# Low parts of the MLP's down weights formed by an adding DMA instead of a VectorE subtraction

## The chip, the cores and the metric

The kernel runs on one core of a Trainium2 chip, in one launch. The metric is device time in microseconds of that core: the median of repeated runs. A profile of one execution gives the order and the durations of the instructions. In the views, PE is TensorE, PEld its weight loads, DVE VectorE, ACT ScalarE, POOL GpSimd and SP SyncE, which here only issues DMAs.

## What is computed

A decoder trunk of two layers over 512 tokens of 1024 channels. Each layer has a token mixer (a linear recurrence with pooling in the first, a convolution module in the second), a cross-attention into 256 memory tokens, and a gated MLP with a short causal convolution. The part that the change touches is the MLP:

```python
def conv_ffn(x, norm, w_up, dw_w, dw_b, w_down):
    h = rms_norm(x, norm) @ w_up
    g = causal_dwconv(h[..., :D_FF], dw_w, dw_b)   # width 3, D_FF = 3072
    u = h[..., D_FF:]
    return (jax.nn.gelu(g) * u) @ w_down
```

It is called once in each layer, and its result is added to the residual stream.

## The kernel before

Activations lie with channels on the 128 partitions and the 512 tokens along the free dimension; `X[c]` is chunk c of 8. All large products keep float32 accuracy by splitting each operand into a high part, rounded to the matmul's fp32r format, and a low part, the remainder. `mm3` then issues three matmuls for each pair of 128x128 weights and 128x512 activations: high by high (L165), high by low (L166), low by high (L167).

Weights come as tiles of 128x1024 float32 (512 KB). `load_w` takes a tile through four steps: SP loads it into one of 3 `raw` buffers; ACT copies it, rounding, into one of 4 `whi` buffers (L159); DVE, or POOL where the caller says so, forms `wlo = raw - whi` in one of 4 `wlo` buffers (L160); PE uses both. A `raw` buffer comes free when the subtraction has read it, a `whi` and a `wlo` buffer when the last matmul of their tile is done. One weight tile is worth 24 matmuls of width 512 in the MLP.

The order on each engine is set at build time by a scheduler that takes the instructions by priority; weight loads carry a priority `AHEAD = 100` in front of their place in the code, so that a tile's load, copy and subtraction stand on their queues ahead of the work of earlier tiles. Every queue is then run in that order, and an instruction that waits holds up all that stands behind it on its engine.

`ffn` runs the MLP in `NG = 6` groups of `GC = 4` channel chunks. `up(c)` makes chunk c: one tile of gate weights, then DVE scales the result (L472), ACT and DVE do the convolution and the GELU (L475, L477, L478), POOL multiplies by the norm's scale (L479); one tile of the other half's weights, whose result DVE multiplies in (L481), and a split of the product. `down(g)` multiplies group g by its down weights: 4 tiles, each for two chunks of `X`, added by DVE (L492). The program's order is four `up`, then `down` of the group before: 8 up tiles, then 4 down tiles, and so on. The first layer ends with a further `down` for the last group, after four tiles for the second layer's attention are loaded; the second layer ends instead with `finish`, which has its own loop and its own `load_w` calls for the last group's 4 down tiles.

Of the kernel before, what the change touches and what calls it, by code (L numbers as in the profile page):

```python
# [10 lines left out]
F32 = mybir.dt.float32  # L11
F32R = mybir.dt.float32r
AF = mybir.ActivationFunctionType
ALU = mybir.AluOpType

P = 128
T = 512
D = 1024
C = D // P
# [4 lines left out]
NG = 6  # L24
GC = CF // NG
EPS = 1e-6
AHEAD = 100
# [28 lines left out]
def trunk(ctx: ExitStack, tc: tile.TileContext, I: dict, out: bass.AP):  # L56
    nc = tc.nc
    V, A, G, PE = nc.vector, nc.scalar, nc.gpsimd, nc.tensor
# [5 lines left out]
    wp = ctx.enter_context(tc.tile_pool(name="w", bufs=4))  # L64
# [8 lines left out]
    def nm(s):  # L73
        uid[0] += 1
        return f"{s}_{uid[0]}"
# [13 lines left out]
    def tmp_f(n=T):  # L89
        return tmp.tile([P, n], F32, tag="tmp", name=nm("tmp"))  # L90
# [9 lines left out]
    def mm_ps():  # L100

        wide[1] += 1
        return aux_ps() if wide[0] and wide[1] % 7 in (2, 5) else main_ps()
# [13 lines left out]
    def col(name, i=0):  # L117
        j = _COL[name] + i
        return par[:, j : j + 1]
# [16 lines left out]
    for t in range(16):  # L136
        G.memset(invt[:, t : t + 1], 1.0 / (t + 1))


    def load_w(src=None, eng=None, raw=None, parts=1, ahead=AHEAD, park=False):  # L140

        with tc.high_priority(0 if raw is not None else ahead):
            if raw is None:
                raw = wp.tile([P, D], F32, tag="raw", name=nm("raw"), bufs=3)
                nc.sync.dma_start(raw, src)
            if park:
                both = [split(raw[:, i : i + T], None, None, eng) for i in (0, T)]
                return [b[0] for b in both], [b[1] for b in both]
            hi = wp.tile([P, D], F32R, tag="whi", name=nm("whi"))
            lo = wp.tile([P, D], F32R, tag="wlo", name=nm("wlo"))  # L150
            n = D // parts
            for i in range(0, D, n):
                split(raw[:, i : i + n], hi[:, i : i + n], lo[:, i : i + n], eng)
        return hi, lo

    def split(src, hi=None, lo=None, eng=None):
        hi = act_r() if hi is None else hi
        lo = act_r() if lo is None else lo
        A.activation(hi, src, AF.Copy)  # L159
        (eng or V).tensor_tensor(lo, src, hi.bitcast(F32), op=ALU.subtract)  # L160
        return hi, lo

    def mm3(ps, w, x, first, last):
        (wh, wl), (xh, xl) = w, x
        PE.matmul(ps, wh, xh, start=first, stop=False)  # L165
        PE.matmul(ps, wh, xl, start=False, stop=False)  # L166
        PE.matmul(ps, wl, xh, start=False, stop=last)  # L167

    def blk(w, i, n=P):
        hi, lo = w  # L170
        if isinstance(hi, list):
            hi, lo, i = hi[i // T], lo[i // T], i % T
        return hi[:, i : i + n], lo[:, i : i + n]
# [100 lines left out]
    def project(w, i, xs):  # L274
        ps = mm_ps()
        for k in range(C):
            mm3(ps, blk(w, k * P), xs[k], k == 0, k == C - 1)
        if Norm.due:
            Norm.due.r = rstd(Norm.due.ss)
            Norm.due = None  # L280
        return ps
# [183 lines left out]
    def ffn(layer, norm, nxt, mem=None):  # L465
        ys = {}

        def up(c):
            ps = project(load_w(I["wup"][(layer * 2) * CF + c]), c, norm.x)
            g = tmp_f(T + 2)  # L470
            G.memset(g[:, :2], 0.0)  # L471
            V.tensor_tensor(g[:, 2:], ps, norm.r, op=ALU.mult)  # L472
            y = tmp_f()
            dw = lambda j: col("f_dw_w", (layer * 3 + j) * CF + c)
            A.activation(y, g[:, 2:], AF.Identity, scale=dw(2), bias=col("f_dw_b", layer * CF + c))  # L475
            for j in (1, 0):
                V.scalar_tensor_tensor(y, g[:, j : j + T], dw(j), y, op0=ALU.mult, op1=ALU.add)  # L477
            A.activation(y, y, AF.Gelu_apprx_tanh)  # L478
            G.tensor_tensor(y, y, norm.r, op=ALU.mult)  # L479
            ps = project(load_w(I["wup"][(layer * 2 + 1) * CF + c]), c, norm.x)  # L480
            V.tensor_tensor(y, ps, y, op=ALU.mult)  # L481
            ys[c] = split(y)

        def down(g):
            for j in range(C // 2):
                w = load_w(I["wdown"][(layer * NG + g) * (C // 2) + j])
                for i in range(2):
                    n = 2 * j + i
                    ps = mm_ps()
                    for k in range(GC):  # L490
                        mm3(ps, blk(w, k * 2 * P + i * P), ys[g * GC + k], k == 0, k == GC - 1)
                    V.tensor_tensor(X[n], X[n], ps, op=ALU.add)  # L492
                    if g == NG - 1:
                        nxt.feed(n)

        for g in range(NG):
            for c in range(g * GC, (g + 1) * GC):
                up(c)
            if g:
                down(g - 1)  # L500
                if mem and g == 1:
                    mem.operand(0)
                    mem.operand(1)
                    mem.outputs()
        if nxt:
            parked = [mem.key_piece(n, park=True) for n in range(KE)]
            down(NG - 1)
            return parked
        else:
            finish([ys[(NG - 1) * GC + k] for k in range(GC)])  # L510

    def finish(y):

        w = [load_w(I["wdown"][(2 * NG - 1) * (C // 2) + j]) for j in range(C // 2)]
        H = T // 2
        for t in (0, H):
            xs, ss, st = [x[:, t : t + H] for x in X], None, stat_ps()[:, :H]
            for n in range(C):
                ps = mm_ps()[:, :H]
                for k in range(GC):  # L520
                    mm3(ps, blk(w[n // 2], (k * 2 + n % 2) * P), blk(y[k], t, H), k == 0, k == GC - 1)
                V.tensor_tensor(xs[n], xs[n], ps, op=ALU.add)
                sq = tmp_f(H)
                A.activation(sq, xs[n], AF.Square)
                if ss is not None and n < C - 1:
                    V.tensor_tensor(sq, sq, ss, op=ALU.add)
                if n >= C - 2:
                    PE.matmul(st, onesf, sq, start=n == C - 2, stop=n == C - 1)
                ss = sq
            r = scale_of(st, H)  # L530
            for n in range(C):
                g = col("final_norm", n)
                if n in (1, 4):
                    A.activation(xs[n], xs[n], AF.Copy, scale=g)
                    G.tensor_tensor(xs[n], xs[n], r, op=ALU.mult)
                else:
                    V.scalar_tensor_tensor(xs[n], xs[n], g, r, op0=ALU.mult, op1=ALU.mult)
                if n % 2:
                    o = out[n - 1 : n + 1, :, t : t + H].rearrange("c p t -> p c t")
                    (nc.sync, A)[n // 2 % 2].dma_start(o, xall[:, n - 1 : n + 1, t : t + H])  # L540
# [340 lines left out]
    raw = [wp.tile([P, D], F32, tag="raw", name=nm("raw"), bufs=3) for _ in range(2)]  # L881
# [97 lines left out]
```

## Time and profile before

| | |
|---|---|
| median of 3 runs | 1494.37 us (1493.18 to 1495.32) |
| the profiled execution's own time | 1493.2 us |
| its span in the profile | 1491.4 us |
| granted TensorE clock, mean over the span | 0.998 |
| PE busy | 1471.6 us (99%), 6982 matmuls |
| DVE busy | 919.2 us (62%) |
| ACT busy | 637.7 us (43%) |
| POOL busy | 201.1 us (13%) |
| DMA | 156.25 MB, mean 105 GB/s |
| weight-tile loads of `wdown` | 48 of 512 KB |

A group row of the profile has the line, the engine, the operation, output and inputs, shapes and count, then busy time and mean duration, then how long the engine stood idle just before such instructions and what ended the wait. A timeline row has the start, the duration, the engine, the line and the operation, with the idle time before it in brackets.

### The profile page before, as it was taken

To read this page: it belongs to the slowest core of one execution; us is meant where nothing else is said; L and a number is where in the kernel's file an instruction comes from. 1 tells how busy PE (TensorE), PEld (TensorE's weight loads), DVE (VectorE), ACT (ScalarE), POOL (GpSimd) and SP (SyncE) were. 2 spreads that over 40 slices of the span, in tenths; PEclk is the share of its full clock that TensorE was granted. 3 is DMA by queue.
4 is the path that set the end of the run, shared out by engine and by line. 5 is a ranking of instruction groups with operands and counts; after the bars stand their busy time and mean duration, and the time that the engine had idled before them with its cause. 6 is when DMAs were issued, how large, how long until landed. Compare 5 with 4: busy or idle time off the path is not lost.

```text
span 1491.4 us, 17877 instructions
## 1 busy us (share of the span) xinstructions
PE 1471.6 (99%) x6982; PEld 1211.2 (81%) x6982; DVE 919.2 (62%) x1230; ACT 637.7 (43%) x891; POOL 201.1 (13%) x227
## 2 busy tenths in 40 slices
PE   8999999999999999999999999999999999999997
PEld 7988788888888888888887666888888888888886
DVE  7877774647655545455666996666565554545556
ACT  7568753435432323323435347444443332323333
POOL 0002300000110101001006862200001010101000
PEclk9999999999999999999999999999999999999999
DMA  7523343213333223333416553321232233333221
GB/s 275 159 87 99 113 127 91 72 37 114 99 99 97 92 95 99 100 99 99 153 46 180 161 150 118 99 86 56 85 99 92 94 97 100 99 99 99 91 79 57
DMA packets 47478, 156.25 MB, mean 105 GB/s; under 512 B 5281, under 2 KB 7329, under 8 KB 47393
## 3 DMA queue, kind: packets, MB, share of 16 engines
q1 hardware_dynamic: 46160, 154.05, 33.4%
q8 instruction: 55, 0.90, 0.2%
q10 hardware_dynamic: 1232, 1.06, 0.2%
q14 instruction: 31, 0.25, 0.1%
HBM read 144.60 MB, written 2.10 MB: 98 GB/s over the span
## 4 chain that ended last, share of the span: by engine, by line
PE 88%; issue 4%; DVE 3%; ACT 2%; POOL 2%; DMA 1%; SPq 0%; DVEq 0%; POOLq 0%; ACTq 0%
PE mm L165 27%; PE mm L166 27%; PE mm L167 27%; PE aux L166 1%; PE aux L165 1%; PE aux L167 1%; PE aux L756 1%; DVE wlo L160 1%; POOL tmp L611 1%; ACT whi L159 1%; DMA raw<-in_wv 1%; PE aux L415 0%; DVE big L587 0%; POOL act L160 0%; DMA big<-in_mem 0%
## 5 line engine op out<-in xcount | busy, mean ns | idle before, releaser
L167 PE MATMUL mm<-act,wlo 128*128 128x512 f32 (+1 forms) x1829 | 705.4, 386 | 2.5 <-DVE wlo L160 2.5
L165 PE MATMUL mm<-act,whi 128*128 128x512 f32 (+1 forms) x1829 | 706.2, 387 | 0.0
L166 PE MATMUL mm<-act,whi 128*128 128x512 f32 (+1 forms) x1829 | 705.4, 386 | 0.4 <-DVE act L160 0.4
L159 ACT ACTIVATE whi<-raw 128x1024 fp32r<-128x1024 f32 x259 | 274.0, 1060 | 575.2 <-PE mm L166 475.7
L165 PEld LDWEIGHTS mm<-act,whi 128*128 128x128 f32 x1829 | 343.7, 188 | 73.9 <-issue 3.3
L167 PEld LDWEIGHTS mm<-act,wlo 128*128 128x128 f32 x1829 | 343.7, 188 | 72.0 <-DVE wlo L160 3.3
L166 PEld LDWEIGHTS mm<-act,whi 128*128 128x128 f32 x1829 | 343.8, 188 | 69.5 <-DVE act L160 1.3
L160 DVE TENSOR_TENSOR wlo<-raw,whi 128x1024 fp32r<-128x1024 f32 x239 | 296.6, 1243 | 65.5 <-ACT whi L159 62.7
L479 POOL TENSOR_TENSOR tmp<-tmp,r 128x512 f32<-128x512 f32 x48 | 62.0, 1292 | 637.5 <-ACT tmp L478 632.6
L492 DVE TENSOR_TENSOR x<-x,mm 128x512 f32<-128x512 f32 x88 | 60.5, 687 | 96.8 <-PE mm L167 96.8
L472 DVE TENSOR_TENSOR tmp<-mm,r 128x512 f32<-128x512 f32 x48 | 33.2, 692 | 125.3 <-PE mm L167 125.2
L481 DVE TENSOR_TENSOR tmp<-mm,tmp 128x512 f32<-128x512 f32 x48 | 33.2, 691 | 95.5 <-POOL tmp L471 87.2
L781 DVE SCALAR_TENSOR_TENSOR aux<-h,par,aux 128x491 f32<-128x491 f32 (+16 forms) x106 | 71.9, 727 | 2.1 <-PE aux L756 1.1
L477 DVE SCALAR_TENSOR_TENSOR tmp<-tmp,par,tmp 128x512 f32<-128x512 f32 x96 | 71.9, 749 | 1.9 <-issue 0.2
L478 ACT ACTIVATE tmp<-tmp 128x512 f32<-128x512 f32 x48 | 30.3, 632 | 95.5 <-DVE tmp L477 95.5
L160 POOL TENSOR_TENSOR wlo<-raw,whi 128x1024 fp32r<-128x1024 f32 x20 | 49.2, 2467 | 123.2 <-ACT whi L159 123.0
L159 ACT ACTIVATE act<-tmp 128x512 fp32r<-128x512 f32 x84 | 52.6, 630 | 23.4 <-DVE tmp L623 7.1
L160 DVE TENSOR_TENSOR act<-tmp,act 128x512 fp32r<-128x512 f32 x84 | 59.9, 716 | 4.1 <-ACT act L159 4.0
L471 POOL MEMSET tmp<- 128x2 f32 x48 | 4.8, 100 | 298.3 <-DVE tmp L195 298.3
L475 ACT ACTIVATE tmp<-tmp,par 128x512 f32<-128x512 f32 x48 | 38.5, 803 | 0.6 <-DVE tmp L472 0.6
L779 POOL TENSOR_TENSOR actf<-actf,tmp 128x499 f32<-128x499 f32 (+7 forms) x28 | 36.3, 1296 | 11.5 <-ACT actf L775 10.2
L166 PE MATMUL aux<-act,whi 128*128 128x512 f32 x79 | 30.8, 389 | 0.0
(214 smaller groups left out, 1290.8 us busy)
## 6 DMA issues: line engine op xcount, KB each, us to landing
raw<-in_wup SPq DMA_DIRECT2D x96, 512.0 KB, 3.5
raw<-in_wdown SPq DMA_DIRECT2D x48, 512.0 KB, 3.6
raw<-in_pw SPq DMA_DIRECT2D x24, 512.0 KB, 4.1
raw<-in_win SPq DMA_DIRECT2D x20, 512.0 KB, 3.6
raw<-in_wv SPq DMA_DIRECT2D x16, 512.0 KB, 5.0
raw<-in_wk SPq DMA_DIRECT2D x16, 512.0 KB, 3.6
raw<-in_wq SPq DMA_DIRECT2D x16, 512.0 KB, 3.6
raw<-in_wo SPq DMA_DIRECT2D x16, 512.0 KB, 3.6
```

The lines of the kernel that those rows point to most:

```text
L159: A.activation(hi, src, AF.Copy)
L160: (eng or V).tensor_tensor(lo, src, hi.bitcast(F32), op=ALU.subtract)
L165: PE.matmul(ps, wh, xh, start=first, stop=False)
L166: PE.matmul(ps, wh, xl, start=False, stop=False)
L167: PE.matmul(ps, wl, xh, start=False, stop=last)
L472: V.tensor_tensor(g[:, 2:], ps, norm.r, op=ALU.mult)
L475: A.activation(y, g[:, 2:], AF.Identity, scale=dw(2), bias=col("f_dw_b", layer * CF + c))
L477: V.scalar_tensor_tensor(y, g[:, j : j + T], dw(j), y, op0=ALU.mult, op1=ALU.add)
L479: G.tensor_tensor(y, y, norm.r, op=ALU.mult)
L492: V.tensor_tensor(X[n], X[n], ps, op=ALU.add)
L779: G.tensor_tensor(z[:, s:], z[:, s:], f[:, s:], op=ALU.add)
L781: V.scalar_tensor_tensor(ps[:, s:], h[:, : T - s], tap(s, c), ps[:, s:], op0=ALU.mult, op1=ALU.add)
```

## The change

A new helper `load_summed` takes the place of `load_w` for the tiles of `down`. It loads `raw` and forms `whi` as before. For the low part, ACT copies `raw` with a factor of -1 into the `wlo` buffer, rounding, which gives minus the high part; then an adding DMA, issued by POOL, adds the unrounded weights onto it in place. Its source is the `raw` tile in the first layer, and the weights in memory, read a second time, in the second layer. `finish` keeps `load_w`.

```diff
+    def load_summed(src, again):
+
+        with tc.high_priority(AHEAD):
+            raw = wp.tile([P, D], F32, tag="raw", name=nm("raw"), bufs=3)
+            nc.sync.dma_start(raw, src)
+            hi = wp.tile([P, D], F32R, tag="whi", name=nm("whi"))
+            lo = wp.tile([P, D], F32R, tag="wlo", name=nm("wlo"))
+            A.activation(lo, raw, AF.Copy, scale=-1.0)
+            G.dma_start(lo, src if again else raw, accum_op=ALU.add)
+            A.activation(hi, raw, AF.Copy)
+        return hi, lo
...
         def down(g):
             for j in range(C // 2):
-                w = load_w(I["wdown"][(layer * NG + g) * (C // 2) + j])
+                w = load_summed(I["wdown"][(layer * NG + g) * (C // 2) + j], layer)
```

It applies to 24 tiles in the first layer (6 groups of 4) and 20 in the second (5 groups of 4). Lines of `ffn` lie 12 further down in the changed kernel (L471 becomes L483, L479 L491). The orders of PE and SP are the same as before, name for name and step for step. What moves is on ACT, POOL and DVE.

On ACT, at the first group's down tiles of the first layer: `whi_3799` to `whi_3901` are the four high parts before, `tmp_3679` and `tmp_3755` the GELU chains of chunks 6 and 7. Before:

```order
L159 ACTIVATE whi_3799<-raw_3797 128x1024
L475 ACTIVATE tmp_3679<-tmp_3676,par 128x512
L478 ACTIVATE tmp_3679<-tmp_3679 128x512
L159 ACTIVATE whi_3833<-raw_3831 128x1024
L159 ACTIVATE act_3717<-tmp_3679 128x512
L159 ACTIVATE whi_3867<-raw_3865 128x1024
L475 ACTIVATE tmp_3755<-tmp_3752,par 128x512
L478 ACTIVATE tmp_3755<-tmp_3755 128x512
L159 ACTIVATE whi_3901<-raw_3899 128x1024
```

And now, where L149 is the high part and L147 the negated copy:

```order
L149 ACTIVATE whi_3799<-raw_3797 128x1024
L147 ACTIVATE wlo_3800<-raw_3797 128x1024
L487 ACTIVATE tmp_3679<-tmp_3676,par 128x512
L490 ACTIVATE tmp_3679<-tmp_3679 128x512
L149 ACTIVATE whi_3834<-raw_3832 128x1024
L147 ACTIVATE wlo_3835<-raw_3832 128x1024
L171 ACTIVATE act_3717<-tmp_3679 128x512
L149 ACTIVATE whi_3869<-raw_3867 128x1024
L147 ACTIVATE wlo_3870<-raw_3867 128x1024
L487 ACTIVATE tmp_3755<-tmp_3752,par 128x512
L490 ACTIVATE tmp_3755<-tmp_3755 128x512
L149 ACTIVATE whi_3904<-raw_3902 128x1024
```

Each down tile's negated copy stands right behind its high part, so one more copy stands ahead of a chunk's GELU chain.

On POOL, at the same place, before:

```order
L471 MEMSET tmp_3752 128x2
L479 TENSOR_TENSOR tmp_3679<-tmp_3679,r_3218 128x512
L471 MEMSET tmp_3992 128x2
L479 TENSOR_TENSOR tmp_3755<-tmp_3755,r_3218 128x512
L471 MEMSET tmp_4068 128x2
```

And now:

```order
L483 MEMSET tmp_3752 128x2
L148 DMA wlo_3800<-raw_3797 128x1024
L491 TENSOR_TENSOR tmp_3679<-tmp_3679,r_3218 128x512
L148 DMA wlo_3835<-raw_3832 128x1024
L483 MEMSET tmp_3996 128x2
L148 DMA wlo_3870<-raw_3867 128x1024
L491 TENSOR_TENSOR tmp_3755<-tmp_3755,r_3218 128x512
L148 DMA wlo_3905<-raw_3902 128x1024
L483 MEMSET tmp_4072 128x2
```

The four adding DMAs now stand among the multiplications of chunks 6 and 7, each waiting there for its tile's negated copy on ACT. In the second layer the same rows read `in_wdown` in place of `raw`. DVE loses the 44 subtractions of these tiles, which stood between the instructions of `up` and `down`.

## The prediction

> **What bounds the kernel now.** First the page's totals, with PE's row of the 40 slices:
>
> ```profile
> PE 1471.6 (99%) x6982; PEld 1211.2 (81%) x6982; DVE 919.2 (62%) x1230; ACT 637.7 (43%) x891; POOL 201.1 (13%) x227
> ...
> PE   8999999999999999999999999999999999999997
> ```
>
> Then PE's own waits (who waited for whom: total, times, longest, in us), of which these two are for low parts of weights:
>
> ```profile
> PE mm L167 <- DVE wlo L160: 3.1, 3, 1.4
> ...
> PE mm L166 <- DVE wlo L160: 1.4, 3, 0.5
> ```
>
> And a table by stage, to see whether PE ever waits where the change works; after the stretch and its length each row has the busy time of five engines, the granted clock and the DMA engines' share:
>
> ```profile
> core 0: us, PE busy (x) PEld busy (x) DVE busy (x) ACT busy (x) POOL busy (x), PEclk, DMA share, GB/s
> 0.00:340.00 340.00, 333.01 (x1612) 279.37 (x1613) 236.84 (x342) 197.05 (x298) 29.64 (x51) 1.00 0.36 116
> 340.00:740.00 400.00, 400.00 (x1766) 331.35 (x1765) 222.01 (x266) 141.47 (x172) 34.45 (x50) 1.00 0.34 105
> 740.00:1060.00 320.00, 316.99 (x1661) 248.19 (x1660) 222.42 (x325) 151.58 (x237) 101.68 (x74) 1.00 0.37 107
> 1060.00:1440.00 380.00, 380.00 (x1678) 314.73 (x1677) 207.49 (x248) 133.08 (x160) 32.10 (x48) 1.00 0.32 100
> 1440.00:1491.40 51.40, 41.60 (x271) 37.52 (x269) 30.49 (x53) 14.51 (x27) 3.21 (x4) 0.94 0.16 52
> ```
>
> PE is the bound. Rows two and four of the table are the two MLPs without their ends: 400.00 of 400 and 380.00 of 380 us busy, at a clock of 1.00. The modelled ends of matmuls can hide very short gaps, but no wait for a subtraction: those are 3.1 and 1.4 us in all, six times, and PE's missing time lies in the other three stretches. So nothing that makes a low part ready earlier in the MLP can bring the end forward; only something that makes it late can move it.
>
> How early a low part is ready is read from the timeline of one down group of the first layer, here ACT (the high parts and two steps of the GELU chain), DVE, POOL and SP.
>
> ```profile
> 632.15 1.06 ACT L159 ACTIVATE whi<-raw 128x1024 fp32r<-128x1024 f32 x1 [3.68 <-PE mm L166]
> 633.12 0.80 ACT L475 ACTIVATE tmp<-tmp,par 128x512 f32<-128x512 f32 x1
> 635.96 0.63 ACT L478 ACTIVATE tmp<-tmp 128x512 f32<-128x512 f32 x1 [2.04 <-DVE tmp L477]
> 637.59 1.06 ACT L159 ACTIVATE whi<-raw 128x1024 fp32r<-128x1024 f32 x1 [1.00 <-PE mm L166]
> ...
> 643.03 1.06 ACT L159 ACTIVATE whi<-raw 128x1024 fp32r<-128x1024 f32 x1 [3.68 <-PE mm L166]
> ...
> 648.48 1.06 ACT L159 ACTIVATE whi<-raw 128x1024 fp32r<-128x1024 f32 x1 [1.01 <-PE mm L166]
> ...
> 653.91 1.06 ACT L159 ACTIVATE whi<-raw 128x1024 fp32r<-128x1024 f32 x1 [3.46 <-PE mm L166]
> ...
> 633.25 1.23 DVE L160 TENSOR_TENSOR wlo<-raw,whi 128x1024 fp32r<-128x1024 f32 x1 [0.23 <-ACT whi L159]
> ...
> 636.67 1.29 POOL L479 TENSOR_TENSOR tmp<-tmp,r 128x512 f32<-128x512 f32 x1 [9.55 <-ACT tmp L478]
> ...
> 634.50 0.33 SPq L145 DMA_DIRECT2D raw<-in_wdown  x1
> ```
>
> The five high parts are D0 to D3, the group's down tiles, and the next up tile. Each waits for PE to release the buffer of the tile four places earlier, so each start marks the end of a tile on PE: 637.59, 643.03, 648.48, 653.91, one tile every 5.44 us. D0's buffer came free at 632.15; three more tiles run before D0, which therefore starts at 648.48. Its low part enters with the third matmul, two of 24 later: 648.48 + 2 x 5.44/24 = 648.93. It was ready at 633.25 + 1.23 = 634.48. That is a cover of 14.4 us, and the same for every tile of the MLP, since every tile keeps this pace.
>
> **The change part by part.** The prices are from these rows of the page:
>
> ```profile
> L159 ACT ACTIVATE whi<-raw 128x1024 fp32r<-128x1024 f32 x259 | 274.0, 1060 | 575.2 <-PE mm L166 475.7
> L160 DVE TENSOR_TENSOR wlo<-raw,whi 128x1024 fp32r<-128x1024 f32 x239 | 296.6, 1243 | 65.5 <-ACT whi L159 62.7
> q1 hardware_dynamic: 46160, 154.05, 33.4%
> raw<-in_wdown SPq DMA_DIRECT2D x48, 512.0 KB, 3.6
> actf<-h SPq DMA_DIRECT2D x32, 256.0 KB, 4.9
> ```
>
> *Removed.* 44 subtractions on DVE, 44 x 1.243 = 54.7 us. DVE is 222.01 of 400 us busy in the first MLP and PE does not wait for it: worth 0.
>
> *Added on ACT.* 44 copies, 44 x 1.06 = 46.6 us, onto 141.47 of 400 and 133.08 of 380 us. The copy for D0 stands ahead of L475, which began at 633.12 and would begin at about 634.2. The chain L475, L477, L478, L479 and L481 of that chunk moves by 1.1 us with it. Behind L481 waits the release of one PSUM bank of five, and five products of two to a tile take over 10 us: 0. If that cover were gone, it would be 1.1 us for each of 22 chunks.
>
> *Added on POOL.* 44 DMA issues. The trace shows none by POOL; SP's issue row has 0.33 us, POOL's own longest step here 1.29 us. I take 1.3. Behind an issue that waits stand L479 and L471 of later chunks. But what D0's issue waits for, its copy, ends at 634.2, before the 636.67 at which L479 could start, and D1's and D3's copies end near 639.7 and 650.6, between two L479. Nothing that PE needs soon is behind them: 0.
>
> *Moved: when the low part is ready.* Call T the time from the end of the negated copy to the landing of the sum, POOL's issue included. High part and copy run back to back, so D0's copy ends at 632.15 + 2 x 1.03, some 634.2, and the sum must land by 648.93: **T up to 14.7 us costs nothing** in the second layer. In the first the adding DMA also holds `raw`. D3's load is issued when D0's tile is let go: in the SP row at 634.50, right behind the subtraction's end at 634.48. It would be issued at 634.2 + T and land 3.6 later. D3's high part could then start at the later of 648.48 and 637.8 + T, its copy end 2.1 after, its sum land T after that; three tiles after its buffer came free its matmuls begin, and the sum is needed at 648.48 + 16.3 + 0.45 = 665.2. So 637.8 + 2.1 + 2T may reach 665.2: **T up to 12.65 us costs nothing** in the first layer.
>
> *What T is.* No row shows an adding DMA. From below: it moves no less than a load of the same tile, 3.6 us. From above: a copy within the on-chip memory, `actf<-h`, takes 4.9 us for 256 KB; two such for 512 KB are 9.8, and twice that, since two operands are read, is 19.6. Near the lower end I take 2 x 3.6 = 7.2, because size, shape and row length are those of the load and two operands are read where the load reads one; with 1.3 for the issue, T = 8.5 us (an estimate), from 4.9 to 20.9. 8.5 lies below both limits, so the sum is 0. The Trainium skill, "Collectives: The Full Stack", section "Part 3: Why 7× under link rate — side-by-side accounting", says that a reduce in the DMA engines runs at half the copy's rate because two sources are read, not because of the addition; by it only the transfer doubles, T would be 3.6 + 1.7 + 1.3 = 6.6 us, and the sum 0 as well; no adding DMA in this trace can confirm it.
>
> *DMA traffic.* 33.4% of 1491.4 us for 154.05 MB is 1.70 us of all 16 engines for one 512 KB tile (0.524 MB). A group of 12 tiles takes 65.3 us and 12 x 1.70 = 20.4 us of the engines; four adds at twice 1.70 bring it to 34. The second read from memory falls in the same account. Room is left: 0.
>
> Sum: 0 us on the profiled execution's own 1493.2 (span 1491.4 and 1.8 around it), which lies 1.2 below the median shown. So the median stays: **1494.4 us**. Its own band, for repeat scatter (1493.18 to 1495.32) and a stray start-up wait of the first adds, is 1492.5 to 1496.5.
>
> **The rivals.**
>
> *The sum lands late (slower).* The place is PE's third matmul of a down tile; it decides from T = 12.65 us in the first layer and 14.7 in the second. At T = 16, D0 is late by 1.3 and D3 of the first layer lands at 637.8 + 2.1 + 32 = 671.9, late by 6.7 against 665.2. That is 6.7 x 6 groups + 1.3 x 5 = 46.7 us, so 1541. At the upper end, 20.9, it is D0 6.2 late, D3 16.5: 16.5 x 6 + 6.2 x 5 = 130 us, so 1624. For it: the on-chip copy at 4.9 us for half the bytes, and that nothing in the trace bounds an add. Against it: it needs T half again above my estimate.
>
> *The adds hold the 16 engines (slower).* If each keeps them for X, four that come every 5.44 us queue from X = 5.44 on. With X = 8 the fourth ends 3 x 2.56 = 7.7 us behind its own time; T alone 1.3 + 8 + 2 (what a load's 3.6 has beyond its 1.70), so 19.0, which is 4.3 over 14.7, in 11 groups 47 us: 1541 again. It begins near X = 6.9, where 1.3 + 6.9 + 2 + 3 x 1.46 = 14.6. For it: the addition's own rate is unknown. Against it: X would be four times a load's 1.70.
>
> *DVE's relief is worth something (faster).* PE's waits for `wlo` are 3.1 + 1.4 = 4.5 us; were all gone, 1489.9. Against it: the table has no PE idle in the stretches where the 44 subtractions are.
>
> **How the numbers follow.** The forecast 0.53; late landing 0.25; engines held 0.18; relief 0.04. A measurement of this kernel can tell about 0.2% (3 us) from no change; both slow cases pass that, so faster 0.04, same 0.53, slower 0.43. The range goes down to 1490, the relief's price. Upward, about half of the two slow cases lies below T = 16.5 or X = 8.2, some 1550; above that about 0.2 is left out. The lower half of T's bounds costs nothing and the top, 1624, stays outside.
>
> **What would show it.** Right: in the changed profile PE still 400.00 of 400 between 340 and 740 us; no PE wait for a DMA on `wlo` in L167's row; the adding DMAs at 5 to 12 us from issue to landing; DVE near 865 us, ACT near 684; 44 POOL issues. Wrong: L167 idle before, with `wlo`'s DMA as releaser, once or more in a group; in the first layer more than in the second if T is the cause (the held `raw`), about alike if it is X; and then ACT's high part waiting for a load instead of PE. A landing median over 12.65 us would break the forecast at the step "what T is".

## The result: 3.4 us slower, lost behind the first layer's last weight tiles

| | before | changed |
|---|---|---|
| median | 1493.49 us (1492.80 to 1495.32, 20 runs) | 1496.89 us (1494.36 to 1500.04, 20 runs) |
| profiled execution, its span | 1493.2, 1491.4 us | 1499.38, 1497.5 us |

The ratio is 1.0023, 95% interval 1.0016 to 1.0029: slower by 0.23%, just past what this measurement can tell from no change. The forecast was no change; the time lies in its range of 1490 to 1550 and 0.4 us above its own band.

The page of the changed kernel, the totals and the adding DMAs' own rows (queue, packets, MB, share; then size and median us from issue to landing):

```profile
PE 1475.5 (99%) x6982; PEld 1213.8 (81%) x6982; DVE 867.0 (58%) x1186; ACT 676.8 (45%) x935; POOL 239.7 (16%) x271
...
q0 software_dynamic: 6336, 23.07, 8.5%
...
wlo<-raw POOLq DMA_DIRECT2D x24, 512.0 KB, 5.5
...
wlo<-in_wdown POOLq DMA_DIRECT2D x20, 512.0 KB, 7.8
```

DVE, ACT and the landings are near where the prediction put them (865, 684, 5 to 12 us). The table by stage of the changed kernel, same columns as before:

```profile
340.00:740.00 400.00, 400.00 (x1766) 331.17 (x1765) 194.20 (x243) 160.97 (x193) 52.77 (x71) 1.00 0.48 130
740.00:1060.00 320.00, 314.69 (x1639) 246.06 (x1638) 217.28 (x319) 149.58 (x234) 103.97 (x77) 0.99 0.39 114
1060.00:1440.00 380.00, 380.00 (x1678) 314.55 (x1678) 186.38 (x228) 152.51 (x183) 48.63 (x67) 1.00 0.47 123
```

PE is still busy for 400.00 of 400 and 380.00 of 380 us: inside the two MLPs nothing was lost. The middle row has lost 2.3 us of PE (316.99 before) and a hundredth of the clock. It is the stretch after the first layer, where the convolution module begins. PE's waits in the changed kernel name the place:

```profile
PE stat L273 <- DVE tmp L223: 2.4, 1, 2.4
PE stat L249 <- ACT actf L804: 2.1, 1, 2.1
```

The second stood in the trace of before too, as L237 with 1.9 us; the first is new. L273 adds up the squares of the residual for the convolution's norm. Four microseconds at a time, before:

```profile
760.00:764.00 4.00, 4.00 (x34) 3.83 (x33) 1.22 (x4) 0.72 (x3) 0.00 (x0) 1.00 0.40 131
764.00:768.00 4.00, 3.99 (x29) 3.34 (x28) 2.11 (x4) 1.00 (x2) 0.00 (x0) 1.00 0.01 4
```

and changed:

```profile
760.00:764.00 4.00, 1.61 (x15) 1.41 (x13) 3.36 (x5) 2.91 (x4) 0.00 (x0) 1.00 0.42 123
764.00:768.00 4.00, 4.00 (x22) 4.00 (x23) 0.60 (x2) 0.57 (x2) 0.00 (x0) 0.57 0.25 101
```

PE waits, and right behind the wait its clock is at 0.57 for one slice. Matching PE's 6982 matmuls of the two traces one by one gives the bill of this execution: 0.6 us from the start-up, 2.3 from this wait, 1.5 from the clock behind it, 1.2 at 902 to 908 us (there the clock falls after the 2.1 us wait, and not after the 1.9 of before), 0.2 in small steps: 5.8 at the end. The median run lost 3.4 us. Only this execution was profiled, but the mean clock of every run is known: 0.997 for the two runs at the median, 0.995 for this one. A phase of 3.4 us at half clock is 0.001 of that mean, so the median runs have, by this estimate, about two phases fewer than the three seen here (start-up, 764, 904 us): they lost mostly the wait. Which phase they kept isn't known.

**Why the squares are late.** Four queues around that place in the changed kernel: SP's load issues, ACT, DVE and PE.

```profile
736.26 0.33 SPq L144 DMA_DIRECT2D raw<-in_wdown  x1
...
739.02 0.33 SPq L157 DMA_DIRECT2D raw<-in_pw  x1
...
741.90 1.06 ACT L149 ACTIVATE whi<-raw 128x1024 fp32r<-128x1024 f32 x1 [6.05 <-DMA raw<-in_wdown]
742.87 1.04 ACT L147 ACTIVATE wlo<-raw 128x1024 fp32r<-128x1024 f32 x1
743.82 0.61 ACT L221 ACTIVATE tmp<-x 128x512 f32<-128x512 f32 x1
747.04 1.06 ACT L171 ACTIVATE whi<-raw 128x1024 fp32r<-128x1024 f32 x1 [2.61 <-PE mm L179]
748.00 0.61 ACT L221 ACTIVATE tmp<-x 128x512 f32<-128x512 f32 x1
...
761.40 0.63 ACT L221 ACTIVATE tmp<-x 128x512 f32<-128x512 f32 x1 [0.41 <-DVE x L504]
...
741.62 0.69 DVE L504 TENSOR_TENSOR x<-x,mm 128x512 f32<-128x512 f32 x1 [2.03 <-PE mm L179]
748.13 1.23 DVE L172 TENSOR_TENSOR wlo<-raw,whi 128x1024 fp32r<-128x1024 f32 x1 [5.82 <-ACT whi L171]
749.27 0.69 DVE L223 TENSOR_TENSOR tmp<-tmp,tmp 128x512 f32<-128x512 f32 x1
...
763.16 1.05 PE L273 MATMUL stat<-onesf,tmp 128*128 128x1 f32 x8 [2.39 <-DVE tmp L223]
```

The same work in the kernel before:

```profile
728.83 0.33 SPq L145 DMA_DIRECT2D raw<-in_pw  x1
...
739.20 0.63 ACT L209 ACTIVATE tmp<-x 128x512 f32<-128x512 f32 x1 [2.66 <-DVE x L492]
...
758.24 0.61 ACT L209 ACTIVATE tmp<-x 128x512 f32<-128x512 f32 x1
...
742.05 1.23 DVE L160 TENSOR_TENSOR wlo<-raw,whi 128x1024 fp32r<-128x1024 f32 x1 [0.23 <-ACT whi L159]
...
760.25 1.05 PE L261 MATMUL stat<-onesf,tmp 128*128 128x1 f32 x8
```

The first load for the convolution is issued at 739.02 instead of 728.83, because `raw` buffers are held by adding DMAs until these land. The end of the first layer is the one place with eight down tiles by adding DMA in nearly a row (the last two groups, four parked tiles between), so the delays add up: the last down tile's load goes out at 736.26, right when an add of 5.7 us from issue to landing lets go of its buffer. ACT then stands idle for 6.05 us until that load lands at 741.9. At 747.04 it waits once more; the row names PE, but the load issued at 739.02 landed at 746.93, and that came last. Behind these two high parts stand the squares of the residual (L221), and on DVE, behind the low part of the same tile (idle 5.82 us), the additions and sums (L504, L223). After 748 additions, squares and sums run one behind the other, and the last square starts at 761.40 instead of 758.24.

### The profile page after: what moved, and what is told of

It is laid out like the page before. It is cut to its first block, busy times and chain, and to the rows that moved or that the text cites. A ratio compares the mean times of both kernels' runs of the same rounds, so it can differ in the third digit from the quotient of the medians.

```text
span 1497.5 us, 17969 instructions
## 1 busy us (share of the span) xinstructions
PE 1475.5 (99%) x6982; PEld 1213.8 (81%) x6982; DVE 867.0 (58%) x1186; ACT 676.8 (45%) x935; POOL 239.7 (16%) x271
## 4 chain that ended last, share of the span: by engine, by line
PE 83%; issue 4%; DVE 3%; ACT 2%; POOL 2%; DMA 0%; DVEq 0%; POOLq 0%; ACTq 0%
PE mm L177 26%; PE mm L179 26%; PE mm L178 26%; PE aux L179 1%; PE aux L178 1%; PE aux L177 1%; PE aux L768 1%; DVE wlo L172 1%; POOL tmp L623 1%; POOL act L172 1%; PE aux L427 0%; DVE big L599 0%; DVE x L549 0%; ACT whi L171 0%; DMA raw<-in_wv 0%
## 5 line engine op out<-in xcount | busy, mean ns | idle before, releaser
L172 DVE TENSOR_TENSOR wlo<-raw,whi 128x1024 fp32r<-128x1024 f32 x195 | 242.6, 1246 | 64.9 <-ACT whi L171 64.3
L491 POOL TENSOR_TENSOR tmp<-tmp,r 128x512 f32<-128x512 f32 x48 | 62.0, 1291 | 459.8 <-ACT tmp L490 454.9
L504 DVE TENSOR_TENSOR x<-x,mm 128x512 f32<-128x512 f32 x88 | 60.3, 686 | 95.6 <-PE mm L179 95.6
L149 ACT ACTIVATE whi<-raw 128x1024 fp32r<-128x1024 f32 x44 | 46.7, 1062 | 81.8 <-PE mm L178 46.5
L483 POOL MEMSET tmp<- 128x2 f32 x48 | 9.7, 202 | 298.2 <-DVE tmp L207 298.2
L147 ACT ACTIVATE wlo<-raw 128x1024 fp32r<-128x1024 f32 x44 | 45.9, 1044 | 2.5 <-DMA raw<-in_wdown 2.5
```

What stands on the lines that cost most here:

```text
L147: A.activation(lo, raw, AF.Copy, scale=-1.0)
L149: A.activation(hi, raw, AF.Copy)
```

## The experiments

**The add reads memory in both layers.** `raw` is then free when ACT has read it.

```diff
-                w = load_summed(I["wdown"][(layer * NG + g) * (C // 2) + j], layer)
+                w = load_summed(I["wdown"][(layer * NG + g) * (C // 2) + j], True)
```

> All 44 adds read the weights from memory, so a raw buffer comes free when ACT's two copies have read it, in the first layer too; ACT's copies, POOL's issues and DVE's relief stay. Seam theory (in the first layer the adding DMA holds raw, the last tiles' and the next weights' loads start about 10 us late, ACT's high parts wait for them at 742 to 750 us with the next norm's squares behind them, and PE waits 2.4 us for the sum and loses about 1.5 us more at a lower clock): about the time of the kernel before, 1493.5, within 1 us; last square near 758, PE's wait at L273 for DVE's tmp gone, clock 1.00 between 764 and 768. Rival, cost of the extra work itself (copies on ACT, traffic, a lower clock over the whole span): 3.4 us above before, as changed, or more, since 24 tiles are read a second time from memory.

1494.11 us, ratio 1.0002 (0.9993 to 1.0011). All 44 adds, all 44 extra copies and 24 more tiles read from memory cost nothing that can be measured; what cost was the held buffer. Its trace has one wait of PE for an add, 0.6 us at the seam, and 0.2 us for the sum. The same slices of this run, with PE at work and the clock at full:

```profile
760.00:764.00 4.00, 4.00 (x32) 3.72 (x30) 3.04 (x5) 2.86 (x3) 0.00 (x0) 1.00 0.10 39
764.00:768.00 4.00, 4.00 (x35) 4.00 (x35) 1.06 (x4) 0.57 (x3) 0.00 (x0) 1.00 0.40 122
```

**The last down group by subtraction again.**

```diff
+                w = load_w(I["wdown"][(layer * NG + g) * (C // 2) + j]) if layer == 0 and g == NG - 1 else load_summed(I["wdown"][(layer * NG + g) * (C // 2) + j], layer)
```

> Only the last down group of the first layer (4 tiles) goes back to the subtraction on DVE; the other 40 adds stay. Seam theory: those four tiles are the ones that stand beside the next weights' loads, so most of the 3.4 us goes: 1493.5 to 1495, with the first load for the convolution module nearer to 729 than to 739 us; a rest of up to 1 us may stay, because the group before it still adds from raw. Rival (extra work or clock over the whole span): 40 of 44 parts of 3.4 stay, 3.1 us above before.

1493.80 us, ratio 0.9999 (0.9991 to 1.0008): taking four of 44 tiles back removes the whole loss.

**Only the last eight down tiles of the first layer by adding DMA.**

```diff
+                w = load_summed(I["wdown"][(layer * NG + g) * (C // 2) + j], layer) if layer == 0 and g >= NG - 2 else load_w(I["wdown"][(layer * NG + g) * (C // 2) + j])
```

> Only the last 8 down tiles of the first layer are formed by the adding DMA from raw; the other 36 go back to the subtraction. Seam theory: the whole 3.4 us from 8 adds, 1496 to 1497.5, with the PE wait of some 2.4 us for DVE's tmp at 760 to 763 us. Rival (cost per add, in traffic, ACT's time or clock): 8 of 44 parts, 0.6 us, 1494.

1497.08 us, ratio 1.0021 (1.0012 to 1.0030): eight adds cost what 44 do. Its waits are not quite those expected:

```profile
PE stat L273 <- DVE tmp L223: 2.1, 2, 1.6
...
PE mm L179 <- DMA wlo<-raw: 1.1, 1, 1.1
```

The longest wait for a sum is 1.6 us here, the one at the seam, and a low part itself came 1.1 us late: the first down tile after the parked ones, whose load had to wait too. Both are the seam's. Behind the 1.6 us the clock stayed at 1.00; this execution's clock fell behind the wait near 900 us, 2.3 us here.

**Only the second layer by adding DMA.**

```diff
+                w = load_summed(I["wdown"][(layer * NG + g) * (C // 2) + j], layer) if layer else load_w(I["wdown"][(layer * NG + g) * (C // 2) + j])
```

> The first layer goes back to the subtraction; the 20 adds of the second layer stay, from memory. Seam theory: the time of the kernel before, 1493.5, within 1 us; PE 380.00 of 380 busy between 1060 and 1440 us. Rival (cost per add): 20 of 44 parts, 1.5 us, 1495, or more if the second read from memory is the dear part.

1493.52 us, ratio 0.9996 (0.9987 to 1.0005). As expected, nothing.

**Low parts of the next weights on POOL.** To learn which queue hurts, the low parts of the convolution's first four tiles leave DVE.

```diff
-        w = [load_w(I["pw1"][n]) for n in (C, 0, C + 1, 1)]
+        w = [load_w(I["pw1"][n], G) for n in (C, 0, C + 1, 1)]
```

> As changed, but the low parts of the convolution module's first four weight tiles are formed by POOL and not by DVE, so that no instruction waiting for a late high part stands on DVE's queue ahead of the residual additions and the sums of squares; the adds, the held raw buffers and the late loads stay as they are, and ACT's queue is the same. Theory (the loss is the head of DVE's queue: 5.8 us idle before L172 at 748.1, additions and sums serial behind it): DVE keeps PE's pace, the wait of PE's L273 for DVE falls from 2.4 to under 1 us, time back to 1493.5 to 1494.5. Rival 1 (ACT's own queue is what holds it: the squares stand behind the same high parts): the wait stays at 2 us or more, 1496 to 1497. Rival 2 (late loads hurt in themselves, through PE needing these weights): another PE wait, for a low or high part, at 765 us or later, and no gain.

1502.75 us, ratio 1.0064 (1.0051 to 1.0076): worse, and the theory that DVE's queue alone is the loss fell. ACT's queue alone is enough to hold the sums up: the second chunk's square still stood behind the high part that waits for the load, and DVE waited 4.75 us for the square. Beside POOL's subtraction DVE's sums were also stretched, from 0.69 to 2.48 us in this row of DVE:

```profile
747.54 2.48 DVE L223 TENSOR_TENSOR tmp<-tmp,tmp 128x512 f32<-128x512 f32 x1 [4.75 <-ACT tmp L221]
```

PE's wait for the sum grew to 5.3 us. Which part of it the stretched sums are, this run can't say.

**The load made later, with the scheduler knowing.**

```diff
+                if late is not None:
+                    G.tensor_copy(raw[:, :1], late[:, :1])
                 nc.sync.dma_start(raw, src)
...
-        w = [load_w(I["pw1"][n]) for n in (C, 0, C + 1, 1)]
+        w = [load_w(I["pw1"][n], late=X[1] if n == C else None) for n in (C, 0, C + 1, 1)]
```

> As changed, but the first weight load of the convolution module is made to wait, by a one-column copy from the residual chunk X[1], until that chunk is final. The load is issued later than in the changed kernel (after 745 instead of at 739 us), and because the scheduler knows of the wait, it puts the squares of chunks 0 to 3 ahead of the high part on ACT, and two sums and two residual additions ahead of the low part on DVE. Theory (queue order on ACT and DVE is what costs, not the lateness of the load): the last square comes back from 761.4 to about 759, PE's wait at L273's line falls from 2.4 to under 1 us, the clock stays 1.00 between 764 and 768, and the time is back at 1493.5 to 1494.5. Rival (the lateness of the load itself costs, or the adds' traffic): 1496.5 or more, since the load is later still.

1502.74 us, ratio 1.0066 (1.0052 to 1.0079): a miss. Four squares stood ahead of the high part as hoped, but two high parts then stood together ahead of the fifth. The first of them waited for the delayed load itself: the new order puts that load behind two others on SP, where it was issued only at 750.52, and it landed at 754.85. On ACT (lines lie 2 further down):

```profile
750.40 0.63 ACT L223 ACTIVATE tmp<-x 128x512 f32<-128x512 f32 x1 [1.36 <-DVE x L506]
754.95 2.01 ACT L173 ACTIVATE whi<-raw 128x1024 fp32r<-128x1024 f32 x2 [3.92 <-DMA raw<-in_pw]
756.87 0.61 ACT L223 ACTIVATE tmp<-x 128x512 f32<-128x512 f32 x1
```

The block was moved, not taken away; PE's wait became 4.5 us. So this run did not separate lateness from order.

**High and low parts of the next weights on POOL.**

```diff
-        A.activation(hi, src, AF.Copy)
+        high.tensor_copy(hi, src) if high else A.activation(hi, src, AF.Copy)
...
-        w = [load_w(I["pw1"][n]) for n in (C, 0, C + 1, 1)]
+        w = [load_w(I["pw1"][n], G, high=G) for n in (C, 0, C + 1, 1)]
```

> As changed, but POOL forms the high and the low parts of the convolution module's first four weight tiles (a rounding copy and a subtraction), so that neither ACT's nor DVE's queue holds an instruction that waits for their late loads; SP's order, the adds and the held raw buffers stay, so the first of these loads should still land near 747 us. Theory (the loss is what stands behind the late high parts on ACT and DVE, not the late load): squares and additions follow PE's pace again, the last square near 758.5 instead of 761.4, PE's wait at L273 from 2.4 to at most 1.5 us (DVE's sums may take 2 us beside POOL's subtractions), clock 1.00 in 764 to 768, time 1493.5 to 1495. Rival (the load's lateness costs by itself, wherever its parts are formed): 1496.5 or more, with a PE wait for one of these tiles or an unchanged wait at L273.

1500.89 us, ratio 1.0051 (1.0037 to 1.0064). The squares did follow PE's pace at first (chunk 2 at 746.74 where the changed kernel has 750.65), with the load landing at 746.95 as there. Then DVE's sums beside POOL's subtractions became the limit:

```profile
746.74 0.64 ACT L221 ACTIVATE tmp<-x 128x512 f32<-128x512 f32 x1 [1.42 <-DVE x L504]
...
756.70 2.63 DVE L223 TENSOR_TENSOR tmp<-tmp,tmp 128x512 f32<-128x512 f32 x1 [0.70 <-ACT tmp L221]
...
756.38 2.40 POOL L172 TENSOR_TENSOR wlo<-raw,whi 128x1024 fp32r<-128x1024 f32 x1
```

PE waited 3.7 us, for another reason than before. Undecided, as far as the time goes.

**The same without a subtraction.** Both copies on POOL, the sum by an adding DMA from memory.

```diff
+            if pool:
+                G.tensor_scalar(lo, raw, -1.0, None, op0=ALU.mult)
...
+            G.tensor_copy(hi, raw) if pool else A.activation(hi, raw, AF.Copy)
...
-        w = [load_w(I["pw1"][n]) for n in (C, 0, C + 1, 1)]
+        w = [load_summed(I["pw1"][n], True, True) for n in (C, 0, C + 1, 1)]
```

> As changed, but the convolution module's first four weight tiles take the added way too, with both copies on POOL (a rounding copy for the high part, a negated one for the low part) and the adding DMA reading memory: nothing for these tiles stands on ACT's or DVE's queue, and POOL runs no two-operand subtraction beside DVE's sums, which took 2.5 to 2.7 us instead of 0.69 in the run before. The MLP's own adds still hold raw, so the first of these loads should land near 747 as in the changed kernel. Theory (what stands behind a high part that waits for a late load): squares and sums at PE's pace, last square near 758.5, PE's wait at L273 under 1 us, clock 1.00 in 764 to 768, time 1493.5 to 1495. Rival (the lateness costs by itself): 1496.5 or more with the wait at L273 unchanged at 2 us or more, or a PE wait for one of these tiles. If DVE's sums are stretched by POOL's one-operand copies too, the wait stays and nothing is decided.

1496.63 us, ratio 1.0021 (1.0012 to 1.0030). The time is a miss, the place is not. PE's waits between 735 and 800 us (lines 3 further down):

```profile
PE aux L286 <- DVE tmp L281: 1.6, 1, 1.6
PE stat L276 <- DVE tmp L226: 0.5, 1, 0.5
PE mm L182 <- DMA wlo<-raw: 0.4, 1, 0.4
```

With the load as late as ever (landed at 746.08) the wait for the sum is 0.5 instead of 2.4 us, and the clock stays at 1.00. So the late load did no harm once nothing that PE needs stood behind it, on ACT or DVE. A new wait of 1.6 us took its place one step on. DVE's next step took 2.28 us instead of 0.68, beside two products on POOL. The changed kernel has these products at 744.91; here they stood on POOL's queue behind the parts of the four tiles. The end of that work on POOL, and DVE's step:

```profile
762.42 3.09 POOL L148 TENSOR_SCALAR wlo<-raw 128x1024 fp32r<-128x1024 f32 x1
765.81 0.90 POOL L151 DMA_DIRECT2D wlo<-in_pw  x1 [0.30 <-POOL wlo L148]
766.44 1.70 POOL L761 TENSOR_TENSOR big<-fold,par 128x384 f32<-128x384 f32 x2
...
766.42 2.28 DVE L281 TENSOR_TENSOR tmp<-ident,rtok 128x512 f32<-128x512 f32 x1
```

One row per kernel, for the first of the convolution's loads and for PE's wait at the sum; all but the last have the parts of these loads on ACT and DVE:

| kernel | load landed, us | PE's wait for the sum, us | ratio to before |
|---|---|---|---|
| before | 733.5 | none | 1 |
| last group by subtraction | 738.6 | none | 0.9999 |
| add from memory | 742.9 | 0.2 | 1.0002 |
| last eight tiles alone | 746.7 | 1.6 | 1.0021 |
| changed | 746.9 | 2.4 | 1.0023 |
| parts on POOL, by adding DMA | 746.1 | 0.5 (and 1.6 behind it) | 1.0021 |

With the parts on ACT and DVE the wait grows from 0.2 to 1.6 us between a landing at 742.9 and one at 746.7; with the parts on POOL a landing at 746.1 leaves 0.5 us of it.

**A second add ahead of each, and the limits on T.** A quarter tile of zeros is added first, and the real add waits for it.

```diff
+    none = cpool.tile([P, D // 4], F32, tag="none", name="none")
+    G.memset(none, 0.0)
...
+            G.dma_start(lo[:, : D // 4], none, accum_op=ALU.add)
             G.dma_start(lo, src if again else raw, accum_op=ALU.add)
```

> Ahead of each adding DMA stands a second one, of zeros onto a quarter of the low part, and the real one waits for it: T grows from about 6.5 (first layer) and 8.7 us (second) by some 4 to 5, to about 11 and 13, still under the limits of 12.65 and 14.7. The prediction's limits: PE stays 400.00 of 400 between 340 and 740 and 380.00 of 380 between 1060 and 1440, nothing is lost inside the MLPs. The seam theory: the loss at the first layer's end grows, since each held raw buffer makes the loads still later: from 3.4 to 5 to 12 us above before. Rival (limits too wide, because POOL's queue is blocked between the two adds or because the engines are shared): PE idle in 340 to 740, more than 10 us in all.

1533.34 us, ratio 1.0258 (1.0243 to 1.0274): far more than expected. T did not grow evenly. POOL's queue stands still between the two issues of a tile, so the four tiles of a group queue behind each other. ACT's negated copies and POOL's issues of one group of the second layer (lines 4 further down):

```profile
1239.21 1.04 ACT L150 ACTIVATE wlo<-raw 128x1024 fp32r<-128x1024 f32 x1
1244.65 1.04 ACT L150 ACTIVATE wlo<-raw 128x1024 fp32r<-128x1024 f32 x1
1250.09 1.04 ACT L150 ACTIVATE wlo<-raw 128x1024 fp32r<-128x1024 f32 x1
...
1245.19 0.86 POOL L152 DMA_DIRECT2D wlo<-in_wdown  x1 [3.77 <-DMA wlo<-none]
...
1253.72 0.87 POOL L152 DMA_DIRECT2D wlo<-in_wdown  x1 [5.49 <-DMA wlo<-none]
...
1261.27 0.87 POOL L152 DMA_DIRECT2D wlo<-in_wdown  x1 [5.75 <-DMA wlo<-none]
```

They landed 7.5, 5.4 and 5.7 us after their issue, so T, from the copy's end, is 12.4, 13.4 and 15.8; D3's was 19.7. PE waited twice in each group, ten times in all:

```profile
PE mm L183 <- DMA wlo<-in_wdown: 19.8, 10, 3.6
PE mm L183 <- DMA wlo<-raw: 7.2, 1, 7.2
```

So D0 and D1, with T up to 14.5, cost nothing, and D2 and D3 did, from T = 15.4 on (the smallest of D2's): the predicted limit of 14.7 holds. The size of the loss fits it too: D2's T less 14.7 is 0.65 to 2.04 us in the five groups, and PE's first wait in each is 0.64 to 1.97. In the first layer T was 7.8 to 14.2 and no down tile waited between 340 and 735 us; the one wait there, 7.2 us, is the first down tile behind the parked ones, at the seam.

**The same with a whole tile of zeros from memory.**

```diff
+            G.dma_start(lo, I["none"], accum_op=ALU.add)
```

> As the run before, but the extra adding DMA takes a whole tile of zeros from memory: T about 0.9 + 7.8 + 0.9 + 5.5 = 15.1 us in the first layer and 17.4 in the second, over both limits. By the prediction's formula: D3 of the first layer lands at 637.8 + 2.1 + 30.2 = 670.1, late by 4.9 against 665.2, times 6 groups 29 us; D0 of the second layer late by 2.7, times 5 groups 13 us; with the seam 45 to 55 us above before, about 1540 to 1550, and PE's L179 waiting for the DMA on wlo. Rival (cover is longer than worked out, so that the steady MLP still loses nothing): under 10 us. Rival (blocked POOL or shared engines make it worse): over 80 us.

1605.22 us, ratio 1.0749 (1.0734 to 1.0764): the rival of the blocked POOL. The tiles follow each other at some 8 us in the first and 10 in the second layer, in place of 5.44, T reaches 18.7 and 27.7, and PE waits 28.3 us for adds from `raw` and 46.9 for those from memory. Most of the rest lies right behind these waits, mostly 1.7 us at a time, where the clock is at half.

No version beat the kernel before: those that take the loss away come back to its time, because PE's MLP had nothing to gain.

## Why the prediction was right and wrong

*DVE's relief is worth 0*: right. DVE fell by 52 us, and the versions without the seam's loss are at 0.9996 to 1.0002.

*Copies on ACT, issues on POOL, traffic: 0*: right inside the MLPs. An issue took 0.87 us for the 1.3 assumed. An add took 8.5% of 1497.5 us over 44, 2.9 us of the 16 engines, 1.7 times a load's 1.70, where twice was assumed. The rule of the Trainium skill, "Collectives: The Full Stack", section "Part 3: Why 7× under link rate — side-by-side accounting", that a reduce runs at half the copy's rate, errs a little to the same side.

*What T is*: estimated at 8.5 us, measured 4.8 to 8.6 but for one add. Adds from `raw` land 5.5 us after their issue and those from memory 7.8. The exception lies at the seam: the add issued at 736.15, beside two loads and two other adds, landed at 746.16.

*The cover, 14.4 us, and T's limit of 14.7*: borne out by the run with two adds. The limit of 12.65 in the first layer, a limit of 25.3 on the T of D0 and of D3 together, wasn't reached in that run: the two make 22.4 at most. The run with whole tiles of zeros went past it (28.1 or more) and lost time there, but D2's T of 16.1 to 17.3 was past 14.7 too, so it doesn't test this limit alone.

*The rivals*: neither low parts late in the MLP nor held engines came about. The slower side came by a mechanism that was not among the rivals, though half of it stood under the signs of "wrong": ACT's high part waiting for a load instead of PE. That the time still lies in the range is luck in this respect: the room above was left for these two rivals, and neither filled it.

**The step that failed** is "the adding DMA also holds `raw`", worked out for the steady group alone. It asked when D3's sum must land for PE's use of it, and found room. It did not ask two things. First, what comes after a group: with eight down tiles close together each load waits for the add three tiles earlier, and the lateness that eight up tiles soak up elsewhere runs on into the next weights, 10 us. Second, what stands behind a late high part on its queue: at the seam it is the squares of the next norm, for which PE has no cover. The prediction did name what was queued behind the new copies and the new issues, in the steady group, and not behind an old instruction that waits longer. The price was 2.4 us of wait and, in this execution, 1.5 us of clock right behind it. The other 1.2 us of clock lie behind the wait near 900 us, which the kernel before has too; no run shows that the seam made it longer.

## What to carry to other kernels

When a step holds a buffer longer, follow that buffer to every place where its users come in another rhythm (the end of a loop, the next stage's first loads), and not only through the steady loop. At such a place look at what stands behind the waiting instruction on each in-order queue; here, taking four tiles out of 44 back removed all that this change cost. When a source can be read from elsewhere, so that the shared buffer goes free at once, a second read from memory may be the cheaper one.

## What the runs showed of the hardware

- *The clock can fall after a wait of 2 us.* In the twelve profiles, outside the start-up and the last 10 us, no wait of PE of up to 1.9 us had a lower clock right behind it, and every one of 2.9 us or more had. Of twenty waits from 2.0 to 2.8 us, fifteen had and five hadn't, among them one of 2.8. In the start-up it also fell behind shorter waits (in the changed kernel at 24 us, behind 0.5 us). Slices of 1 us behind the 2.4 us wait read 0.71, 0.50, 0.50, 0.58, then 1.00: 1.7 us of clock, so 3.4 us at half. The slices of 4 us in the run with a 4.5 us wait, 0.80 and 0.77, make the same 1.7 us. The Trainium skill, "TensorE: Matmul & The Clock Gate", section "What's actually happening", gives half clock and a free-running window of 3.4 us; the half and the length agree. Its section "HAM oscillation — how this bites in real kernels" warns of idle gaps over about 3.4 us; the runs here show that gaps of 2.0 us can be enough.
- *DVE's steps beside POOL.* A 128x512 sum of 0.69 us took 1.3 to 2.7 us beside POOL's copies and subtractions of 128x1024. A sum that starts during a subtraction ends some 0.55 us after it (750.94 and 751.48, 754.85 and 755.40 in the run with both parts on POOL): it waits for the subtraction rather than sharing with it. DVE's step of 2.28 us above likewise ends 0.56 us after POOL's products. Beside POOL's rounding and negated copies the sums took 0.69 to 2.3 us. The Trainium skill, "SBUF — State Buffer", section "Who interferes with whom", says that a DVE instruction with two SBUF inputs contends with a POOL instruction that reads SBUF; the trace agrees. With both parts on POOL, PE's wait was 3.7 us in place of the 2.4 that were to go.
- *Adds hold POOL only for the issue.* 0.87 us each, while a landing takes 5.5 to 7.8. But a second add that waits for the first holds POOL's queue for the whole landing.
